# Loading Q and K in quarters, one quarter per head, in a batched Q K^T kernel

## The chip, the cores and the metric

One core of one Trainium2 chip. The time is that of one execution of the whole program on the device, in microseconds, as the median of several runs. A profile of one such execution says what each engine did: PE (TensorE, matrix products), ACT (ScalarE), DVE (VectorE), POOL (GpSimd), SP (SyncE, here only a queue that issues stores), and the 16 DMA engines that carry all bytes between HBM and SBUF.

## The reference

```python
batch, n_heads, seq, head_dim = 8, 12, 1024, 64
q, k: float32 [8, 12, 1024, 64]
return np.einsum('bhid,bhjd->bhij', q, k).astype(np.float32)
```

For each of 96 heads the 1024 x 1024 score matrix Q K^T is computed, with 64 as the summed dimension. Q and K are 25 MB each; the result is 403 MB in float32, 4 MiB a head.

## The kernel before, in words

The 96 heads are worked through in blocks of 2, 2, 4, 8 and then five times 16 heads (`sizes`, L81; blocks 0 to 8). While block i is computed, block i+1 is brought in and put in order.

*Coming in.* From block 3 on, one whole tensor of a block (Q, then K) is loaded into `x_sb`, one buffer that holds one tensor of a block of 16 heads: 128 partitions, 32 KB in each, 4 MiB. `load` (L162) issues the DMA. Its issuing engine first waits until the casts that read the former contents of `x_sb` are done (`input_busy`, set in `cast_quads` to the last cast). `stream` (L471) lists the loads in order, `next_load` (L477) takes the next one. Who calls it when is in `LOADS` (L87): in block 2 at head 1 after copy 3, in block 3 at head 2 after copy 1, and in every later block at heads 1 and 7 after copy 1, always on ACT's queue. So in block i Q of block i+1 is issued in head 1 and K of block i+1 in head 7.

*Putting in order.* POOL casts the loaded tensor to float16 in four chunks (`cast_quads`, L210): a chunk is four instructions of 32 partitions each, and takes all 128 partitions of `x_sb`. The chunks go into three buffers `half_sb` in turn. DVE transposes each chunk (`transpose_quads`, L231) into `qk_sb`, two sets that alternate from block to block. `to_half` (L503) puts casts into POOL's order as soon as the load has been issued and a buffer is free; the transposes of Q's chunks are placed at heads 3 to 6 of a block, those of K's chunks at heads 10 to 13 (`TURNS`, L85).

*A head* (`scores`, L265) is done in four steps u = 0 to 3: PE multiplies 256 rows of Q with all of K^T into one half of PSUM (two halves in turn), ACT copies that half, 128 x 2048, into an output buffer (L297). After each copy, what `side` holds for this u is put into the engines' orders; this is where loads are issued. After the fourth copy SP issues the store of the 4 MiB head (L310). There are three output buffers `o_sb`, so ACT's first copy of a head waits for the store of the head three before it.

The last head is split (`scores_split`, L316): one half goes out by an indirect DMA, some rows of it and the other half by SP.

SP's stores run in one DMA queue (q1), ACT's loads in another (q10); both feed the same 16 DMA engines.

Of the kernel before, what the change touches and what calls it, by code (L numbers as in the profile page):

```python
# [9 lines left out]
P = 128  # L10
# [53 lines left out]
def kernel(  # L64
# [14 lines left out]
    of = out.rearrange("b h i j -> (b h) i j")  # L79

    sizes = [2, 2, 4, 8] + [16] * ((BH - 16) // 16)  # L81
    PE_BLOCKS, EARLY = 2, 3
    NMAX = max(sizes)
    CHUNK, HALVES = 64 * 32, 3
    TURNS = (3, 4, 5, 6, 10, 11, 12, 13)  # L85
    APART = (16, 48)
    LOADS = {0: {}, 1: {}, 2: {1: 3}, 3: {2: 1}}  # L87

    pool = ctx.enter_context(tc.tile_pool(name="sb", bufs=1))
    psum = ctx.enter_context(  # L90
# [3 lines left out]
    x_sb = pool.tile([P, NMAX * S * D // P], F32, name="x_sb", tag="x")  # L94
# [36 lines left out]
    n, at = S * D // P * 2, 8 * S // 2  # L131
# [8 lines left out]
    input_busy = []  # L140
# [6 lines left out]
    class Block:  # L147
# [11 lines left out]
            self.ready = []  # L159
            self.over = []  # L160

        def load(self, x, eng, landing=None):  # L162
            events = []
            if self.raw[x] is None:
                at = x * self.elems if self.i == EARLY else 0
                self.raw[x] = x_sb[:, at : at + self.elems]
                landing = input_landing[x]
                events = list(input_busy)
            src = flat[x][self.first * S : (self.first + self.N) * S]
            eng.wait(events)  # L170
            dma = eng.eng.dma_start(
                out=self.raw[x], in_=src.rearrange("(p r) d -> p (r d)", p=P)
            )
            self.landed[x].append(landing.start(dma))

# [276 lines left out]
    blocks, first = [], 0  # L452
# [6 lines left out]
    at = 0  # L459
    for b in blocks[:EARLY]:  # L460
# [7 lines left out]
        else:  # L468
            for x in range(2):
                b.load(x, sp, Landing(nc, f"e{b.i}{x}"))  # L470
    stream = [(b, x) for b in blocks[EARLY:] for x in range(2)]  # L471

    casts = [
        (i, c) for i in range(PE_BLOCKS, len(blocks)) for c in blocks[i].chunks()
# [1 line left out]

    def next_load(eng):  # L477
        if stream:
            b, x = stream.pop(0)
            earlier = (b.i, 0) if x else (b.i - 1, 1)  # L480
            assert b.i == EARLY or not any((i, c[0]) == earlier for i, c in casts)
            b.load(x, eng)

    for x in range(2):
        next_load(sp)
# [6 lines left out]
                out=ident,  # L492
                in_=ident,
# [9 lines left out]
    def to_half(last):  # L503
        while casts:
            i, c = casts[0]
            if i > last or (blocks[i], c[0]) in stream:
                return
            if not (rooms if i == PE_BLOCKS else halves).free():
                return
            done = blocks[i].cast_quads(*c)  # L510
            if i == 2:
                early_busy[:] = [done]
            casts.pop(0)

    def transposed(b, s):
        b.transpose_quads(*s)
        to_half(b.i)

    def block(i, heads, regions, w):
        b = blocks[i]  # L520
        nxt = blocks[i + 1] if i + 1 < len(blocks) else None
        for n in heads:
            side = {}
            if nxt and nxt.by_pe:
                if n == 1:
                    side = {
                        u: [
                            lambda x=u // 2: nxt.transpose_rows(
                                x, regions.next(), dve, nc.vector.tensor_copy
                            )  # L530
                        ]
                        for u in (1, 3)
                    }
            elif nxt:
                parts = nxt.chunks()
                at = TURNS if i > EARLY else [m * b.N // len(parts) for m in range(len(parts))]
                some = [s for m, s in zip(at, parts) if m == n]
                side = {0: [lambda s=s: transposed(nxt, s) for s in some]}
            at = LOADS.get(i, {1: 1, 7: 1})
            if n in at:  # L540
                side[at[n]] = side.get(at[n], []) + [lambda: next_load(act)]
            if i == len(blocks) - 1 and n == b.N - 1:
                b.scores_split(n, regions, w)
            else:
                b.scores(n, side, regions, w)
            to_half(i + 2 + (n == b.N - 1))

    for b in blocks[:PE_BLOCKS]:
        for x in range(2):
            b.cast_rows(x)  # L550
    nc.gpsimd.wait_ge(gps.sem, gps.count)
    to_half(2)

    quarters = Ring([ps_all[:, i * S : (i + 1) * S] for i in range(4)])
    for x in range(2):
        blocks[0].transpose_rows(
            x, quarters.next(), (dve, act)[x], (nc.vector.tensor_copy, nc.scalar.copy)[x]
        )
        to_half(2)
    block(0, [0], quarters, 1)  # L560
    halves_ps = Ring([ps_all[:, 2 * S :], ps_all[:, : 2 * S]])
    halves_ps.busy = [quarters.busy[2] + quarters.busy[3], quarters.busy[0] + quarters.busy[1]]
    block(0, [1], halves_ps, 2)
    for i in range(1, len(blocks)):
        block(i, range(blocks[i].N), halves_ps, 2)
# [31 lines left out]
```

## Time and profile before

| | us |
|---|---|
| runs | 1060.77, 1061.27, 1058.94; median 1060.77 |
| the profiled execution | 1060.67, its span 1058.9 |
| PE busy | 702.3 (66% of the span) |
| ACT busy | 695.6 (66%) |
| DVE busy | 435.4 (41%) |
| POOL busy | 358.3 (34%) |
| a store of a head, issue to landing (median) | 21.8 |
| a load of 4 MiB, issue to landing (median) | 25.2 for Q, 23.4 for K |

Bytes: 50.33 MB read from HBM, 402.78 MB written, 428 GB/s over the span. A store lands 21.8 us after its issue because two others are in front of it or beside it in the queue; the pitch from head to head is less than half of that. An engine's idle time is listed with what released it: of ACT's 331.6 us, 286.3 ended when a store gave a buffer back.

### The profile page before, as it was taken

To read this page: it belongs to the slowest core of one execution; us is meant where nothing else is said; L and a number is where in the kernel's file an instruction comes from. 1 tells how busy PE (TensorE), PEld (TensorE's weight loads), DVE (VectorE), ACT (ScalarE), POOL (GpSimd) and SP (SyncE) were. 2 spreads that over 40 slices of the span, in tenths; PEclk is the share of its full clock that TensorE was granted. 3 is DMA by queue.
4 is the path that set the end of the run, shared out by engine and by line. 5 is a ranking of instruction groups with operands and counts; after the bars stand their busy time and mean duration, and the time that the engine had idled before them with its cause. 6 is when DMAs were issued, how large, how long until landed. Compare 5 with 4: busy or idle time off the path is not lost.

```text
span 1058.9 us, 3350 instructions
## 1 busy us (share of the span) xinstructions
PE 702.3 (66%) x1572; PEld 127.4 (12%) x802; DVE 435.4 (41%) x57; ACT 695.6 (66%) x385; POOL 358.3 (34%) x223
## 2 busy tenths in 40 slices
PE   6875754857477747657765756775674777787771
PEld 1111100111011101101110111110110111111110
DVE  2995939029194008539002917600580930000001
ACT  4766755857477748567765856775674777777771
POOL 7926555056280019065005609100822900000000
DMA  9999999999999999999999999999999999999998
GB/s 378 434 424 433 435 431 434 420 423 428 434 431 433 436 417 435 432 433 433 435 418 436 436 427 430 433 436 429 430 428 428 436 434 434 432 429 433 434 431 366
DMA packets 17186, 453.21 MB, mean 428 GB/s; under 512 B 1929, under 2 KB 1929, under 8 KB 2953
## 3 DMA queue, kind: packets, MB, share of 16 engines
q1 hardware_dynamic: 15008, 408.03, 89.5%
q10 hardware_dynamic: 2016, 42.99, 9.8%
q0 software_dynamic: 144, 1.97, 0.4%
q8 instruction: 9, 0.15, 0.0%
q14 instruction: 9, 0.07, 0.0%
HBM read 50.33 MB, written 402.78 MB: 428 GB/s over the span
## 4 chain that ended last, share of the span: by engine, by line
DMA 65%; ACT 15%; PE 8%; DVE 6%; POOL 4%; issue 1%; SPq 0%; ACTq 0%
DMA out_dram<-o_sb 60%; ACT o_sb L297 15%; PE ps_all L439 7%; DVE kT L239 4%; POOL half L220 3%; DMA x_sb<-in_q_dram 2%; DMA x_sb<-in_k_dram 2%; DVE qT L239 1%; DMA o_sb<-in_q_dram 0%; DVE x_sb L345 0%; DVE o_sb L345 0%; PE ps_all L253 0%; POOL qT L191 0%; DVE kT L260 0%; ACT kT L260 0%
## 5 line engine op out<-in xcount | busy, mean ns | idle before, releaser
L439 PE MATMUL ps_all<-kT,qT 64*128 64x512 f16 x1536 | 696.4, 617 | 327.1 <-ACT o_sb L297 310.0
L297 ACT COPY o_sb<-ps_all 128x2048 f32<-128x2048 f32 (+1 forms) x380 | 687.7, 1859 | 331.6 <-DMA out_dram<-o_sb 286.3
L220 POOL CAST half<-x_sb 32x2048 f16<-32x2048 f32 x176 | 332.5, 1889 | 482.7 <-DMA x_sb<-in_q_dram 307.9
L239 DVE STREAM_TRANSPOSE qT<-half 128x2048 f16<-128x2048 f16 x22 | 202.5, 9477 | 274.0 <-POOL half L220 274.0
L239 DVE STREAM_TRANSPOSE kT<-half 128x2048 f16<-128x2048 f16 x22 | 202.4, 9536 | 132.6 <-POOL half L220 132.6
L436 PEld LDWEIGHTS <-qT 64*128 64x128 f16 x768 | 124.0, 162 | 896.3 <-issue 875.9
L345 DVE COPY x_sb<-ps_all 128x2048 f32<-128x2048 f32 x1 | 2.3, 2292 | 174.0 <-PE ps_all L439 174.0
L374 POOL DMA_INDIRECT out_dram<-x_sb,place x1 | 1.2, 1157 | 176.6 <-DVE x_sb L345 176.6
L239 DVE STREAM_TRANSPOSE kT<-kT 128x1024 f16<-128x1024 f16 x2 | 9.3, 4856 | 0.0
L239 DVE STREAM_TRANSPOSE qT<-qT 128x1024 f16<-128x1024 f16 x2 | 9.2, 4782 | 0.0
L220 POOL CAST qT<-o_sb 32x1024 f16<-32x1024 f32 x8 | 8.3, 1036 | 1.1 <-DMA o_sb<-in_q_dram 0.7
L220 POOL CAST kT<-o_sb 32x1024 f16<-32x1024 f32 x8 | 8.3, 1036 | 0.5
L260 DVE COPY qT<-ps_all 128x1024 f16<-128x1024 f16 x2 | 2.4, 1224 | 11.4 <-PE ps_all L253 11.4
L253 PE MATMUL ps_all<-ident,qT 128*128 128x128 f16 x16 | 2.1, 311 | 7.1 <-POOL qT L191 7.0
L297 DVE COPY o_sb<-ps_all 128x1024 f32<-128x1024 f32 x4 | 4.9, 1225 | 4.4 <-PE ps_all L439 4.4
L345 ACT COPY x_sb<-ps_all 128x2048 f32<-128x2048 f32 (+1 forms) x2 | 3.7, 1860 | 2.1 <-PE ps_all L439 2.1
L260 ACT COPY kT<-ps_all 128x1024 f16<-128x1024 f16 x1 | 1.0, 1013 | 5.1 <-PE ps_all L253 5.1
L366 POOL COPY rest_q<-qT 64x8 f16<-64x8 f16 x4 | 0.6, 197 | 9.9 <-DVE kT L239 9.9
L345 DVE COPY o_sb<-ps_all 128x2048 f32<-128x2048 f32 x1 | 2.3, 2292 | 3.7 <-PE ps_all L439 3.7
L191 POOL CAST qT<-o_sb 128x512 f16<-128x512 f32 x4 | 2.3, 614 | 4.0 <-DMA o_sb<-in_q_dram 4.0
L260 ACT ACT_TABLE_LOAD x1 | 1.3, 1283 | 2.8 <-issue 2.8
L260 DVE COPY kT<-ps_all 128x1024 f16<-128x1024 f16 x1 | 1.2, 1225 | 4.4 <-PE ps_all L253 4.4
(18 smaller groups left out, 14.5 us busy)
## 6 DMA issues: line engine op xcount, KB each, us to landing
out_dram<-o_sb SPq DMA_DIRECT2D x95, 4096.0 KB, 21.8
x_sb<-in_q_dram ACTq DMA_DIRECT2D x5, 4096.0 KB, 25.2
x_sb<-in_k_dram ACTq DMA_DIRECT2D x5, 4096.0 KB, 23.4
x_sb<-in_q_dram SPq DMA_DIRECT2D x1, 2048.0 KB, 14.5
x_sb<-in_k_dram SPq DMA_DIRECT2D x1, 2048.0 KB, 18.9
out_dram<-o_sb SPq DMA_DIRECT2D x1, 2048.0 KB, 17.4
o_sb<-in_k_dram ACTq DMA_DIRECT2D x4, 256.0 KB, 5.2
o_sb<-in_q_dram SPq DMA_DIRECT2D x4, 256.0 KB, 5.4
```

Source lines behind the costliest of these rows:

```text
L191: lambda: nc.gpsimd.tensor_copy(out=rows[:, :, h], in_=self.raw[x][:, h * n : (h + 1) * n].rearrange("p (r d) -> p r d", d=D),),
L220: lambda: nc.gpsimd.tensor_copy(out=dst[q0 : q0 + 32].rearrange("p (r d) -> p r d", d=32), in_=raw[32 * b : 32 * b + 32, c * m : (c + 1) * ...
L239: lambda: nc.vector.transpose(out=dst, in_=buf.rearrange("p (r i) -> p r i", i=32)),
L253: lambda: nc.tensor.transpose(t_ps[:, t], rows[:, t], ident),
L260: lambda: copy(out=dst, in_=t_ps.rearrange("c t m -> c m t")), [done]
L297: lambda: (nc.vector.tensor_copy if by_dve else nc.scalar.copy)(out=dst, in_=ps[:, : w * S]),
L345: lambda: (nc.vector.tensor_copy if copier is dve else nc.scalar.copy)(out=dst[:, t * S : (t + w) * S], in_=ps[:parts, : w * S]),
L366: lambda: nc.gpsimd.tensor_copy(out=packed[:, t, 0, :, c], in_=rows[:, t, :, c]),
L374: nc.gpsimd.indirect_dma_start(out=out.rearrange("b h (m t) j -> (b h m) (t j)", t=T), out_offset=bass.IndirectOffsetOnAxis(ap=place_sb, a ...
L436: return nc.tensor.ldweights(stationary, tile_position=(at, to))
L439: return nc.tensor.add_instruction(mybir.InstMatmult(name=nc.get_next_instruction_name(), ins=[nc.tensor.lower_ap(moving), nc.tensor.lower ...
```

## The change

Blocks up to 4 are loaded as before. From block 5 on, Q and K are each loaded by four DMAs. Part `p` of 0 to 3 takes the partitions p, p+4, p+8, ..., 32 of them with 32 KB each, 1 MiB, from the matching rows in HBM. All four count on the same semaphore, and a cast waits for all that were issued into its tensor. The parts are issued on ACT in runs of four heads: of Q of block i+1 in heads 14 and 15 of block i-1 (for block 5: heads 6 and 7 of block 3) and heads 0 and 1 of block i, of K in heads 6 to 9 of block i. The first part of each run comes after the third copy of its head, the others after the fourth and last. A head now issues at most one quarter of a tensor.

```diff
-    PE_BLOCKS, EARLY = 2, 3
+    PE_BLOCKS, EARLY, WHOLE, PARTS = 2, 3, 4, 4
...
-    LOADS = {0: {}, 1: {}, 2: {1: 3}, 3: {2: 1}}
+    LOADS = {0: {}, 1: {}, 2: {1: 3}, 3: {2: 1, 6: 2, 7: 3}}
+    LOADS[4] = {0: 3, 1: 3, 6: 2, 7: 3, 8: 3, 9: 3, 14: 2, 15: 3}
...
-        def load(self, x, eng, landing=None):
+        def load(self, x, eng, landing=None, part=None):
             events = []
-            if self.raw[x] is None:
-                at = x * self.elems if self.i == EARLY else 0
-                self.raw[x] = x_sb[:, at : at + self.elems]
+            if landing is None:
+                if self.raw[x] is None:
+                    at = x * self.elems if self.i == EARLY else 0
+                    self.raw[x] = x_sb[:, at : at + self.elems]
+                    events = list(input_busy)
                 landing = input_landing[x]
-                events = list(input_busy)
             src = flat[x][self.first * S : (self.first + self.N) * S]
+            rows = slice(0, P) if part is None else slice(part, P, PARTS)
             eng.wait(events)
             dma = eng.eng.dma_start(
-                out=self.raw[x], in_=src.rearrange("(p r) d -> p (r d)", p=P)
+                out=self.raw[x][rows], in_=src.rearrange("(p r) d -> p (r d)", p=P)[rows]
             )
...
-    stream = [(b, x) for b in blocks[EARLY:] for x in range(2)]
+    stream = [
+        (b, x, part)
+        for b in blocks[EARLY:]
+        for x in range(2)
+        for part in ((None,) if b.i <= WHOLE else range(PARTS))
+    ]
...
-            b, x = stream.pop(0)
+            b, x, part = stream.pop(0)
...
-            b.load(x, eng)
+            b.load(x, eng, part=part)
...
-            if i > last or (blocks[i], c[0]) in stream:
+            if i > last or any(later[:2] == (blocks[i], c[0]) for later in stream):
...
-            at = LOADS.get(i, {1: 1, 7: 1})
+            at = LOADS.get(i, LOADS[max(LOADS)])
```

## Prediction

> **What bounds the kernel now.** I read the page first, its slices and its queues.
>
> ```profile
> span 1058.9 us, 3350 instructions
> ...
> DMA  9999999999999999999999999999999999999998
> GB/s 378 434 424 433 435 431 434 420 423 428 434 431 433 436 417 435 432 433 433 435 418 436 436 427 430 433 436 429 430 428 428 436 434 434 432 429 433 434 431 366
> ...
> q1 hardware_dynamic: 15008, 408.03, 89.5%
> q10 hardware_dynamic: 2016, 42.99, 9.8%
> q0 software_dynamic: 144, 1.97, 0.4%
> ```
>
> The 16 DMA engines are busy in every slice: stores (q1) plus loads (q10) plus the indirect store (q0) make 99.7% of their span. No compute engine passes 66%. So the end comes when the DMA engines have moved 453 MB, and an edit can only help by making their packets cheaper, or hurt by making them dearer or by letting the queues run dry.
>
> Next the groups with their waits: they show who follows whom.
>
> ```profile
> L439 PE MATMUL ps_all<-kT,qT 64*128 64x512 f16 x1536 | 696.4, 617 | 327.1 <-ACT o_sb L297 310.0
> L297 ACT COPY o_sb<-ps_all 128x2048 f32<-128x2048 f32 (+1 forms) x380 | 687.7, 1859 | 331.6 <-DMA out_dram<-o_sb 286.3
> L220 POOL CAST half<-x_sb 32x2048 f16<-32x2048 f32 x176 | 332.5, 1889 | 482.7 <-DMA x_sb<-in_q_dram 307.9
> ```
>
> ACT stands idle 331.6 us, 286.3 of it for a store to give back an output buffer, and PE waits for ACT. So the time at which ACT resumes on each head marks a finished store, and its pitch is the DMA engines' price of a head. ACT's timeline around the K load of block 6:
>
> ```profile
> 435.82 1.87 ACT L297 COPY o_sb<-ps_all 128x2048 f32<-128x2048 f32 x1 [2.29 <-DMA out_dram<-o_sb]
> 435.87 0.33 ACTq L171 DMA_DIRECT2D x_sb<-in_k_dram  x1
> ...
> 451.57 3.63 ACT L297 COPY o_sb<-ps_all 128x2048 f32<-128x2048 f32 x2 [8.30 <-DMA out_dram<-o_sb]
> ...
> 464.99 3.64 ACT L297 COPY o_sb<-ps_all 128x2048 f32<-128x2048 f32 x2 [5.97 <-DMA out_dram<-o_sb]
> ...
> 474.75 3.64 ACT L297 COPY o_sb<-ps_all 128x2048 f32<-128x2048 f32 x2 [2.31 <-DMA out_dram<-o_sb]
> ```
>
> Without a load the pitch is 9.76 us (504.07 to 543.11 is 39.04 us for four heads). The three heads with this load take 474.75 - 435.82 = 38.93 us, so a 4 MiB load costs 38.93 - 3 x 9.76 = 9.65 us: exactly what its bytes cost, no more than a 4 MiB store. The same subtraction gives for the Q load of block 6 (367.07 to 406.50) 10.15 us, Q of block 7 (543.11 to 582.37) 9.98, Q of block 8 (718.99 to 758.58) 10.31, both later K loads 9.64 to 9.65, and K of block 5 (259.06 to 299.06, where a head took 9.66) 11.0.
>
> **The change part by part.**
>
> *Bytes and packets.* The same 32 MiB in blocks 5 to 8 arrive in the same 1024 packets of 32 KB (one partition's row each; the trace's packet records: 1.213 us each, 1.209 from start to start). Spread over 16 engines, a quarter load gives each engine two packets, a whole load eight. Cost 0, if the 32 rows are spread evenly; otherwise see the third rival.
>
> *24 more DMAs.* Eight loads become 32. In the packet records a DMA ends on each engine with a 4-byte record, which moves the next packet from 1.209 to 1.215 us: 0.006 us. 24 x 0.006 = 0.14 us. From above the price is bounded by everything in a head's pitch that is not its eight packets, 9.76 - 8 x 1.209 = 0.09 us, so 24 x 0.09 = 2.1 us; I take 0.14, because most of the 0.09 belongs to one DMA engine whose store packets run 1.22 to 1.23 us, and it stays with the stores.
>
> [...]
>
> *The load's own dearness.* Over the plain 9.65, the loads of blocks 5 to 8 that ACT's pitch can show cost 0.50 + 0.33 + 0.66 + 1.35 = 2.8 us extra (Q of 6, 7, 8, K of 5). In the packet records this is load packets of 1.3 to 2.4 us instead of 1.213, nearly all on q10, for some microseconds, and in three of these four loads beginning 4 to 9 us after the load's first packet. All of it gone is the best this edit can do: -2.8. All of it kept is 0. If it were a price per load DMA, 2.8 / 8 = 0.35 us each and 24 more would cost +8.4. A quarter load lasts only some 5 us (two of its packets and two store packets on each engine, 4 x 1.21), so part of the build-up should not happen; but the Q of block 8 was dear from its first packets. I take a quarter of it as gone, -0.7, and keep -2.8 and +8.4 as ends.
>
> *Moved waits on ACT.* The first quarter of each run is issued behind a third copy and waits for POOL's last cast out of x_sb; behind it in ACT's order stand the head's fourth copy and the next heads' copies, and SP's store waits for these. Steady state, with head n of a block starting on ACT at 12.2 us a head with a quarter (9.76 + 2.42) and 9.76 without: Q's last quarter is issued at 12.2 + 7.5 = 19.7, and lands about 9 us later (before, 23.4 us for 4 MiB, which is 16 packets of 1.21 us on each engine and 4 us of lead; now 4 packets and the lead). The 16 casts take 31.1 us (timeline of POOL), so they end near 60. Head 6's third copy ends at 63.4 + 5.7 = 69: no wait, 9 us to spare. K's last quarter is issued at 107.5, lands at 116.6, casts end at 148, and head 14's third copy ends at 157: 9 us to spare. The K transposes end at 116.6 + 7.8 + 36.8 = 161, and the next block starts at 175.6. Cost 0.
>
> In block 3 there is a real wait, for K of block 4 is cast late:
>
> ```profile
> 142.97 31.14 POOL L220 CAST half<-x_sb 32x2048 f16<-32x2048 f32 x16 [23.32 <-DMA x_sb<-in_k_dram]
> ```
> ```profile
> 164.70 3.64 ACT L297 COPY o_sb<-ps_all 128x2048 f32<-128x2048 f32 x2 [0.17 <-PE ps_all L439]
> 170.62 3.64 ACT L297 COPY o_sb<-ps_all 128x2048 f32<-128x2048 f32 x2 [2.29 <-DMA out_dram<-o_sb]
> ```
>
> Head 6's third copy ends at 166.6, the casts at 174.1: ACT stops for 7.5 us, and head 6's store goes out at about 176.4 instead of 168.3. At 170.62 the store of head 4 has just ended; head 5's, long issued, runs from there to 180.4. So the queue never empties, the two quarters issued there add 4.8 us of work, and the wait costs 0. Without that queue it would cost 7.5. Block 4 starts on the K transposes as before, which the change does not touch.
>
> *Issue time.* 24 x 0.33 us on ACT, behind last copies, inside the 2.3 us that ACT waits on every plain head: 0.
>
> *Sum.* 0 + 0.14 - 0.7 + 0 = -0.56. The profiled execution took 1060.67 us (its span 1058.9 and 1.8 around it), next to the median 1060.77. 1060.67 - 0.56 = 1060.1 us.
>
> **The rivals.**
>
> *All the dearness goes* (short bursts never build it up). For: late onset in three of those four loads. Against: Q of block 8, and what makes packets dear is not seen in the trace. 1060.67 + 0.14 - 2.8 = 1058.0.
>
> *Slower: each start of a load has a price on every engine.* Its place is the moment when q10 joins q1: at the start of the Q load of block 5 and the K load of block 8 store packets of 1.5 to 2.2 us appear. Against: the K loads of blocks 6 and 7 have none. At 0.35 us a start 1060.67 + 8.4 = 1069; it decides (over 0.2%) from 2.1 / 24 = 0.09 us a start.
>
> *Slower: 32 partitions, every fourth, are spread badly over the engines,* so that two share what one had. Nothing in the trace has this shape. Each quarter could then cost up to two packets more, half of that on average by chance of overlap: 32 x 1.21 = 39 us, 1099. Against: the stride takes rows from the whole range of partitions. The Trainium skill, DMA: Bandwidth & Descriptors, section The descriptor swizzle, says that engines take partitions in groups of four in a transfer of 128; by that a stride of four leaves each engine its own rows, but the page says it only for 128.
>
> *Slower: a DMA's lead lies open.* From 23.4 us less 16 packets of 1.21 a load has 4 us of lead before its first packet; if the engines stood still for it, 24 more would cost 96 us, 1157. Against: with a load in the queue the three heads above cost 9.65 us more, the bytes alone. [...]
>
> *A wait that comes late:* the 9 us to spare are worked out, not seen; 7.5 us lost once, without cover, gives 1068.
>
> **How the numbers follow.** The forecast 0.60, with its own range 1058 to 1063 (inside it 0.05 to either side beyond the bound); all dearness gone 0.20; a price per start 0.12; bad spread 0.05; open lead 0.01; late wait 0.02. A measurement of this kernel can tell about 0.2%, 2.1 us, from no change. Faster by more: 0.05 + 0.20 = 0.25. Slower by more: 0.05 + 0.12 + 0.05 + 0.01 + 0.02 = 0.25. Same: 0.50. The range runs from 1057, a little below the best case 1058.0, to 1066, which holds half of the starts' price and leaves out the rest.
>
> **What would show it.** Right: the slices' GB/s and the 9.76 us pitch unchanged, a head with a quarter at 12.1 to 12.3 us, three waits of ACT on POOL at most, one of them in block 3, POOL's casts starting about 9 us after the last quarter's issue, and q10 with 24 x 16 = 384 more packets of 4 bytes. Heads with a quarter above 12.6 us would mean a price per start; above 13.4, a bad spread. Wrong it would be if a slice other than the first and last fell below 410 GB/s, or ACT waited for POOL in every block.

## The result and the profile after

The changed kernel takes 1069.93 us (median of 6 runs, 1067.56 to 1072.15), the kernel before, in the same session, 1061.02 (1058.94 to 1062.57): ratio 1.0084 with a 95% interval of 1.0065 to 1.0103, so it is 8.9 us slower. The forecast was 1060.1, the range up to 1066. The profiled execution took 1069.29 us, 8.6 more than the one profiled before.

The page of the changed kernel, its slices and queues, and below them two of its DMA issue lines (median us from issue to landing at the end):

```profile
span 1067.5 us, 3374 instructions
...
DMA  9999999999999999999999999999999999999997
GB/s 375 434 437 433 434 435 425 411 432 431 425 429 433 417 426 433 419 416 433 428 425 429 432 414 428 433 424 425 434 424 424 425 435 432 435 432 434 432 433 325
...
q1 hardware_dynamic: 15008, 408.03, 89.3%
q10 hardware_dynamic: 2400, 42.99, 9.8%
...
L442 PE MATMUL ps_all<-kT,qT 64*128 64x512 f16 x1536 | 696.4, 617 | 332.2 <-ACT o_sb L300 321.2
L300 ACT COPY o_sb<-ps_all 128x2048 f32<-128x2048 f32 (+1 forms) x380 | 687.5, 1859 | 336.9 <-DMA out_dram<-o_sb 291.6
...
x_sb<-in_q_dram ACTq DMA_DIRECT2D x16, 1024.0 KB, 11.8
x_sb<-in_k_dram ACTq DMA_DIRECT2D x16, 1024.0 KB, 11.7
```

The DMA engines are still busy everywhere, with the same 453 MB. No engine works longer than before (ACT's copies 687.5 us against 687.7), and ACT's idle time for a store grew by only 5.3 us, to 291.6. What changed is the rate: compare, in the table by stage, the last column (GB/s) and the one before it (the DMA engines' busy share), first of the kernel before:

```profile
200.00:400.00 200.00, 131.06 (x290) 23.44 (x145) 73.52 (x8) 131.25 (x73) 67.88 (x36) 1.00 1.00 429
400.00:600.00 200.00, 135.12 (x299) 24.05 (x149) 97.94 (x11) 134.90 (x75) 83.27 (x45) 1.00 1.00 430
600.00:850.00 250.00, 163.00 (x360) 29.13 (x180) 115.21 (x14) 163.62 (x90) 92.85 (x60) 1.00 1.00 432
850.00:1020.00 170.00, 127.35 (x282) 22.66 (x140) 7.47 (x1) 127.26 (x70) 0.58 (x4) 1.00 1.00 433
```

then of the changed kernel:

```profile
200.00:400.00 200.00, 128.91 (x285) 23.03 (x142) 73.58 (x8) 128.17 (x71) 66.03 (x35) 1.00 1.00 425
400.00:600.00 200.00, 132.68 (x293) 23.66 (x146) 96.10 (x11) 133.62 (x75) 84.22 (x45) 1.00 1.00 427
600.00:850.00 250.00, 163.76 (x362) 29.30 (x181) 95.70 (x11) 163.49 (x90) 76.24 (x42) 1.00 1.00 426
850.00:1020.00 170.00, 125.64 (x278) 22.34 (x138) 28.90 (x4) 126.43 (x70) 17.73 (x24) 1.00 1.00 433
```

From 200 to 850 us, where quarters are loaded, 0.2 x 4 + 0.2 x 3 + 0.25 x 6 = 2.9 MB fewer were moved, which at 433 GB/s is 6.7 us; where no quarter comes (from 850 on) nothing is lost. The engines were busy all the time: their packets got dearer, no queue ran dry.

ACT's timeline of the changed kernel around K of block 6 shows the heads (start, duration, work, and in brackets the wait before it):

```profile
428.01 3.63 ACT L300 COPY o_sb<-ps_all 128x2048 f32<-128x2048 f32 x2 [2.19 <-DMA out_dram<-o_sb]
...
431.84 0.48 ACTq L174 DMA_DIRECT2D x_sb<-in_k_dram  x1
...
438.94 3.63 ACT L300 COPY o_sb<-ps_all 128x2048 f32<-128x2048 f32 x2 [3.48 <-DMA out_dram<-o_sb]
...
451.35 3.64 ACT L300 COPY o_sb<-ps_all 128x2048 f32<-128x2048 f32 x2 [4.96 <-DMA out_dram<-o_sb]
...
465.22 3.64 ACT L300 COPY o_sb<-ps_all 128x2048 f32<-128x2048 f32 x2 [6.41 <-DMA out_dram<-o_sb]
...
475.02 3.63 ACT L300 COPY o_sb<-ps_all 128x2048 f32<-128x2048 f32 x2 [2.35 <-DMA out_dram<-o_sb]
...
487.12 3.63 ACT L300 COPY o_sb<-ps_all 128x2048 f32<-128x2048 f32 x2 [4.64 <-DMA out_dram<-o_sb]
```

The pitches are 10.93, 12.41, 13.87, 9.80 and 12.10 us: five heads with a whole K load in 487.12 - 428.01 = 59.11 us. Before, three heads with a load and two plain ones took 38.93 + 2 x 9.76 = 58.45.

*Where the time sits.* The trace's packet records say it more finely. A 32 KB packet takes 1.213 us; of each that took over 1.26 us I count what lies above 1.213, sum it, and divide by the 16 engines. I call this the excess of a run; packets of other sizes are not in it. Before it is 1.2 us on stores and 3.7 on loads, after 7.0 on stores and 3.6 on loads. The time of all packets together, per engine, went from 1057.2 to 1063.4 us. The records name no engine; I take a packet to stand, on one engine, behind the packet at whose end it starts. So matched, 5.0 of the 5.9 us of new excess on stores are in store packets just ahead of a quarter's first packet: 46 to 48% of these last over 1.26 us, with a mean of 0.18 to 0.20 us too much over all of them, by the way of matching. Of the quarter's own packets the first is 0.07 us too long in the mean, the second 0.04. Ahead of a whole load, before, the store packet was about 0.1 us too long, in 17 to 20% of cases; load by load it was 0.51, 0.03, 0.08, 0.00, 0.00, 0.00, 0.03 and 0.13 us. So the store packet that an engine carries just before a quarter's first packet is often prolonged.

*And the rest.* 6.2 us of 8.6 are packet time. ACT's last wait for a store before the end fell at 1026.83 instead of 1022.04, 4.8 us later, and the remaining 3.8 us arose behind it: the last slice moves 325 GB/s instead of 366. In the packet records the 16 engines end on average 6.2 us later (1072.18 after 1066.02, on the records' own clock), the last of them 8.5 us later, and first and last lie 8.0 us apart instead of 3.5. The engines have fallen unevenly behind, and the last store ends with the slowest one.

### The profile page after: what moved, and what is told of

Read it like the earlier page. It is cut to its first block, busy times and chain, and to the rows that moved or that the text cites. A ratio compares the mean times of both kernels' runs of the same rounds, so it can differ in the third digit from the quotient of the medians.

```text
span 1067.5 us, 3374 instructions
## 1 busy us (share of the span) xinstructions
PE 702.3 (66%) x1572; PEld 127.4 (12%) x802; DVE 435.7 (41%) x57; ACT 695.4 (65%) x385; POOL 357.8 (34%) x223
## 4 chain that ended last, share of the span: by engine, by line
DMA 65%; ACT 15%; PE 8%; DVE 6%; POOL 4%; issue 1%; SPq 0%; ACTq 0%
DMA out_dram<-o_sb 60%; ACT o_sb L300 15%; PE ps_all L442 8%; DVE kT L242 4%; POOL half L223 3%; DMA x_sb<-in_k_dram 2%; DMA x_sb<-in_q_dram 2%; DVE qT L242 1%; DMA o_sb<-in_q_dram 0%; DVE x_sb L348 0%; DVE o_sb L348 0%; PE ps_all L256 0%; POOL qT L194 0%; DVE kT L263 0%; ACT kT L263 0%
## 5 line engine op out<-in xcount | busy, mean ns | idle before, releaser
L300 ACT COPY o_sb<-ps_all 128x2048 f32<-128x2048 f32 (+1 forms) x380 | 687.5, 1859 | 336.9 <-DMA out_dram<-o_sb 291.6
## 6 DMA issues: line engine op xcount, KB each, us to landing
x_sb<-in_q_dram ACTq DMA_DIRECT2D x16, 1024.0 KB, 11.8
x_sb<-in_k_dram ACTq DMA_DIRECT2D x16, 1024.0 KB, 11.7
```

The source lines that it names most:

```text
L300: lambda: (nc.vector.tensor_copy if by_dve else nc.scalar.copy)(out=dst, in_=ps[:, : w * S]),
```

## The experiments

Words used below: a *burst* is all parts of a tensor issued one behind the other at the old places (heads 1 and 7). The excess is that of one profiled run. Its repetition can be seen in two pairs of profiles, whose only difference is the end of the kernel: 4.8 and 4.0 us for the kernel before, 10.6 and 10.6 for the changed one. Letters in the expectations: A is a price at each start of the load queue, C the place of the issue within a head, T a price of each load DMA that has few packets for each engine, L the load's large first packets as the cause.

**1. Quarters in a burst** (from the changed kernel). 32 DMAs remain, the load queue starts 8 times only.

```diff
-    LOADS = {..., 3: {2: 1, 6: 2, 7: 3}}
-    LOADS[4] = {0: 3, 1: 3, 6: 2, 7: 3, 8: 3, 9: 3, 14: 2, 15: 3}
+    LOADS = {..., 3: {2: 1}}
+    LOADS[4] = {1: 1, 7: 1}
-                side[at[n]] = ... + [lambda: next_load(act)]
+                side[at[n]] = ... + [lambda: next_load(act)] * many   # 4 from block 4 on
```

> The same 32 quarter loads of 32 partitions, but the four of a tensor issued back to back at the old places (heads 1 and 7, behind the second copy), so that the load queue starts 8 times and not 32. Theory A (each start of the load queue beside running stores costs about 8.9 / 24 = 0.37 us): 1061, as before. Rival B (each DMA of this shape costs, wherever it stands): 1070, as with the change. Rival C (the place behind the last copy costs, where the load meets the border of two stores): 1061.

1073.59 us, ratio 1.0125 (1.011 to 1.014), excess 12.8 us. Each of the four quarters' first packets pays again: the store packet ahead of it is 0.35, 0.24, 0.19 and 0.22 us too long in the mean. A load now lasts 24 to 25 us instead of 18 to 20. The waits of ACT in this run:

```profile
ACT o_sb L300 <- DMA out_dram<-o_sb: 283.7, 84, 11.9
ACT o_sb L300 <- PE ps_all L442: 43.5, 101, 10.3
ACT o_sb L300 <- issue: 11.7, 6, 3.7
```

The third line is new: ACT is held in issuing DMAs for 11.7 us in all. So spreading the quarters over heads isn't the harm. But the run does not clear the start of the load queue. Between two packets of one DMA an engine does one store packet in most cases; between the last packet of one quarter and the first of the next it does two in 299 of 381 cases, so the load queue misses a turn there and starts anew. At these borders the store packet ahead of the quarter is 0.26 us too long in the mean; at the 75 borders with one store packet between, 0.03.

**2. Whole loads later** (from the kernel before): behind the last copy instead of the second.

```diff
-            at = LOADS.get(i, {1: 1, 7: 1})
+            at = LOADS.get(i, {1: 3, 7: 3})
```

> The kernel before, with its whole loads moved from behind the second to behind the fourth copy of heads 1 and 7. Theory A: 8 starts as before, 1061. Rival B: 1061. Rival C: about 8 x 0.37 = 3 us more, 1064.

1060.69 us, 1.0007 (0.9999 to 1.0016), excess 3.5: the place costs a whole load nothing that shows.

**3. Quarters earlier** (from the changed kernel): all behind the second copy of their heads.

```diff
-    LOADS = {..., 3: {2: 1, 6: 2, 7: 3}}
-    LOADS[4] = {0: 3, 1: 3, 6: 2, 7: 3, 8: 3, 9: 3, 14: 2, 15: 3}
+    LOADS = {..., 3: {2: 1, 6: 1, 7: 1}}
+    LOADS[4] = {0: 1, 1: 1, 6: 1, 7: 1, 8: 1, 9: 1, 14: 1, 15: 1}
```

> The changed kernel with every quarter behind the second copy of its head, not behind the third or fourth. Theory A: 32 starts, 1070. Rival B: 1070. Rival C: 1061.

1073.43 us, 1.0136 (1.0119 to 1.0152), excess 9.9. It did not get better; the place is not the cause.

**4. Whole loads in SP's queue** (from the kernel before): stores and loads in one queue.

```diff
-                side[at[n]] = ... + [lambda: next_load(act)]
+                side[at[n]] = ... + [lambda: next_load(act if i < 4 else sp)]
```

> The kernel before, with the whole loads of blocks 5 to 8 issued by SP in the queue of the stores, in front of the same head's store, so that they stand in line and no second queue starts. Theory A: the 8 starts and most of the dear packets go, 1058 to 1060. Rivals B and C: 1061. If the later landing (some 20 us behind two stores) holds up POOL and SP, 1065 or more, and waits of SP for POOL would show it.

1062.99 us, 1.0023 (1.0012 to 1.0034), excess 4.1, all now in the one queue q1. What dearness whole loads have doesn't come from two queues taking turns. Where the 2.5 us of time come from was not traced.

**5. Quarters by columns, in a burst** (from the changed kernel): all 128 partitions with 8 KB of each row.

```diff
-            rows = slice(0, P) if part is None else slice(part, P, PARTS)
+            n = self.elems // PARTS
+            cols = slice(None) if part is None else slice(part * n, part * n + n)
...
+    LOADS[4] = {1: 1, 7: 1}     # burst as in 1
```

> As the burst run, but the quarters are cut by columns: each of the four DMAs takes all 128 partitions and 8 KB of each row, eight packets of 8 KB on every engine instead of two of 32 KB. Smaller packets (0.309 us for 8 KB, four for 1.213) add about 8 x 8 x 0.024 = 1.5 us by themselves. Theory B1 (each further load DMA has a price, about 13 / 24 = 0.5 us in a burst, whatever its shape): 1074 or more. Theory B2 (the price is that of the 32 strided rows): 1062.

1075.68 us, 1.0136 (1.0121 to 1.0152), with an excess of only 1.6 us: packets of 8 KB hardly stall the stores. But they are dear themselves, by 7.6 us for each engine over their usual 0.309 us, which the excess leaves out. And a Q load lasts 48 to 51 us, since about one 8 KB packet goes through per 32 KB store packet; its casts come late, ACT waits for them before it can issue K, and the stores run dry: the engines stand idle for 6 to 9 us at the first of these K loads, 1 to 4 at the second, up to 2 at the third, some 11 us in all. The time of this run says nothing of the price.

**6. Tiny quarters added** (from the kernel before): 32 more DMAs of 32 partitions, every fourth, but with 512 B of each row, in heads 4, 5, 6 and 10 to 14 of blocks 4 to 7, into a buffer that nobody reads.

```diff
+        landing.start(
+            eng.eng.dma_start(out=tiny[part:P:4], in_=src[part:P:4, :128])
+        )
...
+            if 4 <= i <= 7 and n in (4, 5, 6, 10, 11, 12, 13, 14):
+                side[3] = side.get(3, []) + [lambda: tiny_load(act)]
```

> The kernel before with 32 further DMAs of the quarters' shape (32 partitions, every fourth) but 512 bytes a row instead of 32 KB, into a buffer that nobody reads, behind the last copy of heads 4 to 6 and 10 to 14 of blocks 4 to 7, away from the whole loads. Their bytes are 0.5 MB in all, about 1.3 us. Theory B1, and B2 if the price lies in the descriptors: 1060.5 + 1.3 + 32 x 0.3 to 0.5 = 1071 to 1078. Theory B3 (the price comes with the rows' 32 KB, not with the DMA): 1062.

1061.96 us, 1.0011 (1.0002 to 1.002), excess 3.3. Store packets ahead of a tiny packet are 0.001 us too long, 0.2% of them over 1.26 us. The page of this run has the added packets, under an unchanged rate:

```profile
DMA packets 18721, 453.73 MB, mean 428 GB/s; under 512 B 2440, under 2 KB 3464, under 8 KB 4488
...
q10 hardware_dynamic: 3552, 43.52, 9.9%
```

So neither the number of DMAs, nor their 32 rows at a stride of four, nor the start of the load queue beside stores has the price by itself: all 32 together cost 1.1 us, with an interval of 0.2 to 2.1. The price needs larger packets.

**7. Halves in a burst** (from the changed kernel): two DMAs of 64 partitions, every second.

```diff
-    PE_BLOCKS, EARLY, WHOLE, PARTS = 2, 3, 4, 4
+    PE_BLOCKS, EARLY, WHOLE, PARTS = 2, 3, 4, 2
...
+    LOADS[4] = {1: 1, 7: 1}     # burst as in 1
```

> As the burst run, but two DMAs of 64 partitions (every second) for each tensor: 16 load DMAs in blocks 5 to 8, 8 more than before. Theory B1: 1060.5 + 8 x 0.5 = 1065. Theory B2: between 1061 and 1074, by how far 64 rows behave like 32.

1062.36 us, 1.0015 (1.0006 to 1.0024), excess 5.1. The store packets ahead of the second halves show no excess (0.00 us), though in 52 of 128 cases the load queue misses a turn there too: 8 more DMAs cost 1.5 us together where 24 more in (1) cost 13.1.

**8. Neighbouring partitions, in a burst** (from the changed kernel).

```diff
-            rows = slice(0, P) if part is None else slice(part, P, PARTS)
+            rows = slice(0, P) if part is None else slice(32 * part, 32 * part + 32)
...
+    LOADS[4] = {1: 1, 7: 1}     # burst as in 1
```

> As the burst run, but each quarter takes 32 neighbouring partitions (0 to 31, 32 to 63, ...) instead of every fourth. Theory B1: 1074, as the burst. If the spread of rows over the engines matters (third rival of the prediction), this is the worse spread and ends at 1085 to 1110; if a stride in the rows is what costs (a form of B2), 1061.

1102.61 us, 1.0387 (1.0373 to 1.0401), 29 us above the burst with the stride of four. The page of this run:

```profile
GB/s 380 436 432 429 430 434 435 339 389 418 374 430 433 427 347 434 389 398 431 434 404 377 432 370 403 432 434 374 390 436 361 414 431 434 431 433 436 427 436 341
...
q10 hardware_dynamic: 2400, 42.99, 12.4%
```

Here it is the load packets themselves: 89% of those of blocks 5 to 8 last over 1.26 us, the mean of all is 0.58 us too much, 37 us of excess in q10, whose share rose from 9.8 to 12.4% with the same bytes. In the changed kernel that share is as before (9.8%). The stride of four avoids this, and what the change costs is another thing.

**9. Halves apart** (from the changed kernel): two DMAs per tensor in separate heads, so the load queue starts 16 times.

```diff
+    PE_BLOCKS, EARLY, WHOLE, PARTS = 2, 3, 4, 2
+    LOADS = {..., 3: {2: 1}}
+    LOADS[4] = {0: 3, 1: 3, 6: 3, 8: 3}
```

> Halves as in the run with two DMAs of 64 partitions, but the two stand apart: behind the last copies of heads 0 and 1 (Q) and 6 and 8 (K), so that the load queue starts 16 times. Theory S (a price for each start whose loads don't follow on another DMA's, about 0.35 us): 1060.5 + 8 x 0.35 = 1063.5. Theory T (the price is that of DMAs with only two packets for each engine): 1061 to 1062, as with the halves together.

1065.28 us, 1.0042 (1.0028 to 1.0055), excess 8.3. Halves pay when they stand apart (0.6 us for each of 8 more starts), and hardly when one follows the other (7).

**10. Quarters in SP's queue** (from the changed kernel).

```diff
-                side[at[n]] = ... + [lambda: next_load(act)]
+                side[at[n]] = ... + [lambda x=n: next_load(sp if i >= WHOLE or x >= 6 else act)]
```

> The changed kernel with the quarters issued by SP, in the queue of the stores and in front of the same head's store. Theory Q (the price comes from two queues taking turns on an engine, where a store packet is held while the load's first packet is awaited): 1061 to 1063, as the whole loads on SP. Theory T: 1070 or more, wherever the quarters are queued.

1078.80 us, 1.0179 (1.0165 to 1.0193), excess 13.6. The price doesn't vanish with the second queue: quarters pay in the stores' own queue too. A part of the time is a new wait, in which stores stand behind a waiting load; SP's queue in this run:

```profile
SPq L174 <- POOL half L223: 41.5, 8, 14.2
```

**11. Parts of 64 rows with 16 KB each, in a burst** (from the changed kernel): four packets per engine and DMA instead of two, of half the size.

```diff
+            rows = slice(0, P) if part is None else slice(part % 2, P, 2)
+            n = self.elems // 2
+            cols = slice(None) if part is None else slice(part // 2 * n, (part // 2 + 1) * n)
...
+    LOADS[4] = {1: 1, 7: 1}     # burst as in 1
```

> As the burst run, four DMAs of 1 MiB for each tensor, back to back, but each takes 64 partitions (every second) and half of each row, so four packets of 16 KB on every engine instead of two of 32 KB. Packets of 16 KB (0.612 us, two for 1.213) cost 0.1 us in all. If the price goes with the number of packets that a DMA gives each engine (theory T): 1061 to 1063. If it goes with the DMA or with its 1 MiB: 1073.

1069.49 us (1064.82 to 1076.09), 1.009 (1.0056 to 1.0124), excess 9.1, which leaves out 0.7 on the parts' own 16 KB packets. With four packets each, as the halves have, the parts still pay: the bare number of packets isn't the criterion.

**12. Quarters by columns, one per head** (from the changed kernel): the column slices of (5) at the change's places.

> The changed kernel, one quarter per head at the same places, but cut by columns: 128 partitions and 8 KB of each row, eight packets of 8 KB on every engine. By theory T 1060.5 + 1.5 (smaller packets) = 1062; by a price for each start or each DMA 1070 or more. A quarter takes about 12 us here and lands some 7 us later, which the waits of ACT for POOL should still bear.

1069.19 us (1066.02 to 1074.53), 1.0103 (1.0078 to 1.0129), excess 3.8, and 0.2 more on the 8 KB packets. Few dear packets, but a quarter lands 17.7 us after its issue instead of 11.8, and ACT waits for POOL 16.1 us. Confounded, like (5).

**13 and 14. A plain end.** The last head is done like every other one, in the kernel before (13) and in the changed one (14).

```diff
-            if i == len(blocks) - 1 and n == b.N - 1:
-                b.scores_split(n, regions, w)
-            else:
-                b.scores(n, side, regions, w)
+            b.scores(n, side, regions, w)
```

> The kernel before with its last head done as every other head, without the split that takes work from the DMA engine that lags. It should lose what the split gains, 1063 to 1067. It is the partner of the next run.

> The changed kernel with the same plain last head. If the 8.9 us of the change are all work added to every DMA engine, it stands 8.9 us over its partner. If some 3 us of them come from the end, where the split helps an engine that is no longer the last one, it stands only 5 to 6.5 us over its partner.

13: 1062.37 us, 1.0018 (1.0009 to 1.0027). 14: 1069.28 us, 1.0092 (1.0074 to 1.0109). The split end is worth 1.9 us (0.0018 x 1060) in the kernel before, and nothing that shows in the changed one (9.2 us above the kernel before without it, 8.9 with it). Between the two plain ends the change costs 6.9 us, and the packet time per engine differs by 6.85 (1063.23 to 1056.38). So of 8.9 us some 2 are the end's share, or 1 if the ratios are compared (1.0092 / 1.0018 = 1.0074, 7.8 us). The interval is as wide as this share. The records speak for it: with a plain end the 16 engines end 6.1 us apart in the kernel before and 6.3 in the changed one; with the split end it is 3.5 in the one and 8.0 in the other.

**15. Columns with enough lead** (from the changed kernel): as (12), but K's quarters begin in heads 5 and Q's in head 13 of the block before, so that the casts needn't come late.

```diff
+    LOADS = {..., 3: {2: 1, 6: 3, 7: 3}}
+    LOADS[4] = {0: 3, 1: 3, 5: 3, 6: 3, 7: 3, 8: 3, 13: 3, 14: 3, 15: 3}
+    LOADS[5] = {0: 3, 5: 3, 6: 3, 7: 3, 8: 3, 13: 3, 14: 3, 15: 3}
```

> The quarters by columns, one per head, moved up by one head (heads 13, 14, 15, 0 for Q and 5 to 8 for K) so that their later landing holds nobody up. Theory L (the price is the wait for a load's first packet, which a packet of 8 KB meets sooner than one of 32 KB): 32 starts and yet 1062, the smaller packets' 1.5 us over before. Theory S (a price for each start, whatever the packet): 1070 or more.

1065.35 us (1062.36 to 1072.86), 1.0052 (1.0032 to 1.0072). The excess is 2.8 us, with the 0.8 on 8 KB packets 3.6, less than the kernel before has, with four times its DMAs. But the waits did not go:

```profile
ACT o_sb L302 <- POOL half L225: 29.7, 5, 11.4
```

The issues now wait for the casts that free `x_sb`. What remains of the time can't be divided between these waits and anything else.

**16. Quarters in twos** (from the changed kernel): two quarters one behind the other, at the places of (9).

```diff
+    LOADS = {..., 3: {2: 1}}
+    LOADS[4] = {0: 3, 1: 3, 6: 3, 8: 3}
+                side[at[n]] = ... + [lambda: next_load(act)] * many   # 2 from block 4 on
```

> Quarters of 32 partitions, every fourth, as in the change, but issued in twos, behind the last copies of heads 0 and 1 (Q) and 6 and 8 (K): 16 starts of 2 MiB each, 32 DMAs. Theory S: 1065, as the halves apart. Theory T (each DMA with only two packets for an engine pays, also right behind another): 1070 to 1074.

1073.87 us, 1.0127 (1.011 to 1.0143), excess 11.6. Bytes and places are those of (9), each half merely cut into two quarters, and it is 8.6 us slower. The second quarter of a pair pays as well (store packets ahead of it 0.14 us too long). So a quarter right behind another adds its own price. But as in (1), the load queue misses a turn at most of these borders: where two store packets stand between (250 cases) the one ahead is 0.18 us too long, where one does (59 cases) it is not. A price of each quarter DMA and a price of each new start of the load queue are not told apart by this run.

**17 and 18. A small DMA ahead** (from the kernel before). If only the first packet of a load stalls a store and a small one doesn't, a small slice of columns ahead of the rest might make whole loads cheaper: 8 KB of each row, then 24 KB (17), or 2 KB, then 30 KB (18).

```diff
+            cols = (slice(None), slice(0, 2048), slice(2048, self.elems))[0 if part is None else 1 + part]
...
+    LOADS[4] = {1: 1, 7: 1}     # both at the old place
```

> The kernel before, each load of blocks 5 to 8 as two DMAs of 128 partitions back to back at the old places: first 8 KB of each row, then the other 24 KB. Theory L (a load pays for large packets whose data are awaited when its stream begins): the first DMA's small packets cover the second, the dear packets of the whole loads (4.8 us a DMA engine in the trace of before) mostly go, 1058 to 1060 after 0.4 us for smaller packets. Theory T: 1061, no gain. If the longer load (some 10 us) makes ACT wait for POOL: above 1062.

> The same with 2 KB first and 30 KB after. Theory L: 1058 to 1060, if the first packets need only be small; 1061, if it is the large packets behind them that pay.

17: 1063.68 us, 1.0026 (1.0017 to 1.0035), excess 3.6, with that of the 24 KB packets (1.6) 5.2. 18: 1062.10 us, 1.0005 (0.9997 to 1.0014), excess 2.4, with that of the 30 KB packets (2.0) 4.4, against 4.8 in the kernel before. So the excess hardly changed, and there is no gain in time. No version tried beats the kernel before.

Excess and time side by side, for all kernels in which the loads' rows are 32 KB and SP waits for nothing new:

| | load DMAs of blocks 5 to 8 | excess, us | above before, us |
|---|---|---|---|
| before | 8 | 4.8 | 0 |
| 2, later | 8 | 3.5 | 0.2 |
| 6, 32 tiny ones added | 8 | 3.3 | 1.1 |
| 7, halves, burst | 16 | 5.1 | 1.5 |
| 9, halves apart | 16 | 8.3 | 4.9 |
| the change | 32 | 10.6 | 8.9 |
| 3, quarters early | 32 | 9.9 | 13.0 |
| 16, quarters in twos | 32 | 11.6 | 13.8 |
| 1, quarters, burst | 32 | 12.8 | 13.1 |
| 8, neighbouring rows, burst | 32 | 47.1 | 41.8 |

Among the first four, within 1.5 us, the excess says nothing of the time; below them more excess goes with more time, but 3 and 16 stand out. 1, 3 and 16 lose 5 to 8 us more than their excess over the kernel before, the change 3. The packet records show where this arises: the 16 engines end on average 9.0, 6.5 and 7.3 us later than before, but the last of them 12.7, 12.4 and 11.6 us later. First and last lie 9.0 to 9.8 us apart in these three runs. What spreads the engines was not tried.

## Why the prediction was wrong

**The step that failed** is the term "the load's own dearness", taken as -0.7 us between -2.8 and +8.4. It reckoned with dear load packets, said to build up over a long load, so that short loads would have fewer. They did not get fewer: the excess of load packets was 3.7 us before and 3.6 after. What changed is something that the forecast put at nothing and had only in its upper end and a rival, a price at the beginning of a load. It sits in the store packet ahead of a load DMA with large packets, and quarters have four beginnings instead of one: the excess of store packets went from 1.2 to 7.0 us. In packet time the term came out at about +6 instead of -0.7, with 1 to 2 us more at the end of the kernel. The upper end, "a price per load DMA, 0.35 us each", was right in kind: 8.9 / 24 = 0.37 us by the time, 6.2 / 24 = 0.26 by the packets. That 0.35 lies so close to 0.37 is luck: it was worked out from the loads' own dear packets, which stayed as they were, and the 0.37 contains the end's share.

**The rival that came true** is "each start of a load has a price on every engine", 1069, given 0.12. Its number was right, by the same luck. Its place ("the moment when q10 joins q1") fits the records of the changed kernel, and those of (1) and (16), where the load queue misses a turn before most quarters. But it is not the whole: starts with tiny packets don't pay (6), missed turns between halves don't (7), and in (10) quarters pay within the stores' own queue. The evidence held against it, that K loads of blocks 6 and 7 had no dear packets, was read as "starts are free". It showed only that loads of eight packets an engine can start free.

**The end.** The prediction treated the end as fixed. Engines that lag unevenly (8.0 us apart instead of 3.5) make a last head that was cut to suit one lagging engine lose its use: by (13) and (14) 1 to 2 us, with an interval as wide, a term that was missing.

**What held.** *Bytes and packets*, cost 0 by an even spread: q10's share is unchanged at 9.8%, and the 384 predicted extra packets are there (2400 - 2016). *24 more DMAs*, 0.14 with an upper bound of 2.1: in (6) 32 added DMAs cost 1.1 us, interval 0.2 to 2.1. *Moved waits on ACT*: 7.5 us predicted once, in block 3, at no cost; the waits of ACT in the changed kernel:

```profile
ACT o_sb L300 <- POOL half L223: 9.9, 2, 7.2
```

The longest, 7.2 us, ends in block 3 at 173.86, and the slices around it keep the pace. *Sizes that were off without harm*: a quarter lands after 11.8 us, not 9, and its issue takes 0.48 us of ACT, more than the 0.33 of a whole load; both stayed covered. *The plain pitch* became 9.68 us instead of 9.76. The likely reason, not shown, is that the one slow engine of before had set it and that in the changed kernel others are behind it; the pitch then says less of what the mean engine pays. *No inner slice under 410 GB/s*: the lowest is 411. That mark was too coarse for a loss of 1%, while the mark set for heads (above 12.6 us) did speak: 13.87.

**The other rivals.** "Bad spread", 1099, was a real danger with its price nearly right: 32 neighbouring rows gave 1102.61 (8). The change's stride avoids it. Those rows don't sit on fewer engines: with the packets matched as above, nearly every quarter of (8) gives each of the 16 engines two packets. Why these take longer, the records don't show. "A DMA's lead lies open", 1157, is excluded by (6). The Trainium skill, DMA: Bandwidth & Descriptors, in its section on the anatomy of one DMA, fits about 2.0 us fixed for each DMA that GpSimd issues. The 32 tiny ones of (6) were issued by ACT beside a busy store queue and added 1.1 us in all; no run here shows the figure for GpSimd. "All the dearness goes", 1058, is not what the packets show: that of the loads stayed at 3.6 us, and that of the stores grew.

**What stays open.** Whether the price belongs to each load DMA or to each new start of its queue: in (1) and (16) the two go together, and (10) has a price without a second queue. Why a missed turn costs between quarters and not between halves (7): the number of packets doesn't explain it (11). And why the store packet ahead of a new load's large packet is prolonged: the records show where and how long, not why.

## What to carry to other kernels

When DMA engines are the bound, count not bytes alone but how often a load begins beside a full store queue: here four loads of 1 MiB in place of one of 4 MiB cost 0.26 us of DMA time for each extra one, and 0.37 us in all, while tiny loads cost almost nothing (0.03 us each). A price that shows at some starts of before and not at others is a reason to give that rival more weight, not less: of the eight loads of before, three had a store packet 0.08 to 0.51 us too long ahead of them, and multiplying their number by four is the very edit that finds out. Look also at what the end of the kernel was tuned for; a change in the middle can undo it.

## What the runs showed that was not expected

- 32 neighbouring partitions instead of every fourth cost 29 us in 32 loads (1102.61 against 1073.59): load packets of 32 KB took 1.88 us in the median instead of 1.213.
- Packets of two queues take turns one by one in most cases, whatever their size: in (5) a Q load of 8 KB packets beside 32 KB store packets lasted 48 to 51 us, where 32 KB packets take 18 to 21.
- ACT can be held in issuing: with four quarters issued one behind the other it lost 11.7 us in 6 waits (1), with parts of 64 rows 22.7 us (11), of which some 3 were a wait for casts.
- Two load DMAs issued one behind the other don't run on without a break: between quarters the load queue missed a turn on its engine in 299 of 381 cases (1).
